# Other places for the conv blocks' exit from PSUM, for table loads and copies of ScalarE, and for the output's scaling, in a four-layer decoder trunk

## The chip, the cores and the metric

The kernel runs on one core of one Trainium2 chip. The metric is the device time of one execution in microseconds, the median of several runs. A core has five engines with an instruction row of their own, each of which works through its row in order: TensorE (PE: matmuls), VectorE (DVE), ScalarE (ACT), GpSimd (POOL) and SyncE (SP, which here issues DMAs). They share data in SBUF and, for matmul results, in PSUM, and wait for one another through semaphores.

## The reference

What is computed is one inference step of a trunk of four layers, for 256 prompt tokens and 8 sample tokens with the same weights, in float32. Layers 0 and 3 have a short gated conv as mixer, layer 1 a pooling over several windows, layer 2 a Conformer conv; each mixer is followed by an MLP with squared ReLU. The change lies in the Conformer conv and in the last norm.

```python
def layer_norm(x, g, b):
    xf = x.astype(jnp.float32)
    mu = jnp.mean(xf, axis=-1, keepdims=True)
    var = jnp.mean(jnp.square(xf - mu), axis=-1, keepdims=True)
    y = (xf - mu) * lax.rsqrt(var + EPS)
    return (y * g.astype(jnp.float32) + b.astype(jnp.float32)).astype(x.dtype)
...
def conformer_conv_mixer(xn, state, w_pw1, b_pw1, conv_w, conv_b, ln_g, ln_b, w_pw2, b_pw2):
    ag = jnp.einsum('bld,de->ble', xn, w_pw1) + b_pw1
    a, g = jnp.split(ag, 2, axis=-1)
    buf = jnp.concatenate([state, a * jax.nn.sigmoid(g)], axis=1)
    z = causal_dwconv(buf, conv_w) + conv_b
    z = layer_norm(z, ln_g, ln_b)
    y = jnp.einsum('ble,ed->bld', jax.nn.silu(z), w_pw2) + b_pw2
    return y, buf[:, -(CONV_C_W - 1):]
...
    return rms_norm(x, norm_final_g), jnp.stack(new_a), jnp.stack(new_b), jnp.stack(new_c)
```

## The kernel before

Channels lie on the 128 partitions, so the 1024 channels are 8 blocks, and the 264 tokens (256 + 8) lie along the free axis. Every weight matrix comes from HBM as units of 1024 x 256 (`wst`). ScalarE rounds a piece of a unit to fp32r (`whi`, line 119), then VectorE or GpSimd subtracts it from the original (`wlo`, line 120, on the engine in `lo_engine`), and TensorE multiplies three times (`mm`, lines 160 to 162). `pump` puts these two steps in between other work. The order of all instructions on each engine is the order in which the Python code issues them (`manual_schedule`).

In `mixer_c` (line 827) the first pointwise product and the GLU give 8 blocks `gb`. The depthwise conv over 31 taps is split: blocks 0 to 3 are done on VectorE, tap by tap, in a PSUM accumulator (`do_taps`, line 858; the last tap and the bias come first, as a scaled copy of ScalarE, line 901), and blocks 4 to 7 on TensorE, as 64 steps `conv_step` (line 926) over matrices `mats` that hold the taps. Each of these four blocks leaves two half results in PSUM, `pairs`. `leave` (line 951) takes a block out: ScalarE copies the two halves that lie on the other partitions (`over`), VectorE adds them to the own halves (line 960). `apart` (line 967) subtracts an estimated mean, on GpSimd or VectorE, squares on ScalarE, and lets GpSimd add the blocks up into `dsum` and `qsum`; blocks 3 and 7 stay apart. Calls of all these are placed by the step number n in the loop over the 64 steps (lines 1015 to 1044).

After the loop `token_sums` (line 994) sums over the channels with matmuls against a matrix of ones, 28 or 56 columns wide: `dsum`, `qsum`, then block 3 and its square, then block 7 and its square. From these come the mean and the inverse root of each token, spread to all partitions by two small products (`wide` and `scale`, `to_channels`). `keep_clock(n)` issues n matmuls of ones by ones with no use for the result, called warm-up here; each is two passes in the trace. Then the second pointwise product starts as a `wave` over three units, whose first step needs the first normed block (`normed`, `gated`). A table load stands on ScalarE wherever the function set changes (Sigmoid, Sqrt); `root_table` asks for Sqrt early.

At the end of the kernel the squares of the last layer are summed per token, `rsqrt` gives a scale per token, and three row blocks `ys` of 128 tokens are scaled in two halves and sent out (lines 1285 to 1307).

Of the kernel before, what the change touches and what calls it, by code (L numbers as in the profile page):

```python
# [11 lines left out]
ALU = mybir.AluOpType  # L12
# [14 lines left out]
def decoder_trunk(ctx: ExitStack, tc: tile.TileContext, i, o):  # L27
# [136 lines left out]
    def psum():  # L164
        return pmm.tile([P, 512], F32, tag="mm", name="mm")
# [661 lines left out]
    def mixer_c(ready):  # L827
# [61 lines left out]
        def evac_a(e, ps):  # L889
            t1 = ps[:, :T]  # L890
            nc.vector.tensor_tensor(out=t1, in0=t1, in1=r, op=ALU.mult)
            nc.vector.scalar_tensor_tensor(
                out=gb[e][:, 30:], in0=t1, scalar=col("bpw1", e), in1=sg.pop(e), op0=ALU.add, op1=ALU.mult
            )
            later.append(lambda: out_rows.put(e, gb[e][:, 30 + T - P:]))

            def rest():
                if e < PE0:
                    if e < 3:
                        zb[e] = psum()  # L900
                    nc.scalar.activation(
                        z(e), gb[e][:, 30:30 + SEQ], AF.Identity, scale=col("ccw", 30 * 8 + e), bias=col("cb", e)
                    )
                    todo[e] = list(range(30))
                elif e < NB - 1:
                    double(e)
                if e in (0, 1, 2, 4):
                    make_mat()
                    make_mat()
                sample_sum(e)  # L910
                do_taps(4)

            return rest
# [24 lines left out]
        def first_mean():  # L938
# [9 lines left out]

            return means

        def leave(e):


            over = tmp.tile([P, SEQ], F32, tag="t1", name="over")
            for s in range(2):
                own, other = (slice(h * HALF, (h + 1) * HALF) for h in (s, 1 - s))
                nc.scalar.copy(over[own], pairs[e, s][other, 1:SEQ + 1])
            for s in range(2):
                own = slice(s * HALF, (s + 1) * HALF)
# [54 lines left out]
        total, done = sum(len(v) for v in todo.values()), 0  # L1014
        for n, step in enumerate(steps):
            conv_step(*step)
            if n == 15:
                leave(4)
                double(NB - 1)
            if n < 16:  # L1020
                make_mat(nc.scalar if n % 4 == 3 else nc.gpsimd)
            if n >= 20 and n % 3 == 0:
                run_later(1)
            want = total * max(0, n - 3) // 58
            done += do_taps(want - done, not (todo[0] or todo[1]))
            if n == 58:
                root_table()
            for at, e in ((33, 5), (49, 6)):
                if n == at:
                    leave(e)  # L1030
            if n == 8:
                assert not (todo[0] or todo[1])
                means = first_mean()
            if n == 16:
                ss = means()
            if n == 20:
                nc.vector.tensor_scalar_mul(mu, ss, 1.0 / (P * some))
# [12 lines left out]
        lo_engine[0] = nc.vector  # L1050
        pump(len(background))
        lag[0] = 0
        widths = (28, 56)
        sums = [pst.tile([P, T], F32, tag="st", name="sums"), psum()]
        few = tmp.tile([P, 4, 3], F32, tag="rs", name="few", bufs=1)
        md, v, root, rz = (few[:, k] for k in range(4))
        wide = psum()
        warm = ptp.tile([P, 512], F32, tag="tp", name="warm")
        keep_clock(5, warm)
        token_sums(sums[0], widths[0], 0, "d")  # L1060
        token_sums(sums[1], widths[1], 0, "q")
        token_sums(sums[0], widths[0], 1, "d3")
        token_sums(sums[1], widths[1], 1, "q3")
        token_sums(sums[0], widths[0], 2, "d7")
        token_sums(sums[1], widths[1], 2, "q7")
        dq = [
            ps[:, 0:9 * w].rearrange("p (b r w) -> p b r w", r=3, w=w)[:, :, :, 0] for ps, w in zip(sums, widths)
        ]
# [217 lines left out]
    for n, sq in enumerate((acc, last_square)):  # L1286
        for b, c0 in enumerate(starts):
            c = n * 3 + b
            nc.tensor.matmul(ss[:, c:c + 1], sq[:, c0:c0 + P], ones[:, 0:1], start=True, stop=True)
    run_later(NB)  # L1290
    rt = tmp.tile([P, 3], F32, tag="rt", name="rt", bufs=1)
    v, s = root_tiles(3)
    mean(v, ss[:, 0:3])
    nc.vector.scalar_tensor_tensor(out=v, in0=ss[:, 3:6], scalar=1.0 / D, in1=v, op0=ALU.mult, op1=ALU.add)
    rsqrt(v, s, rt)
    for b in range(3):
        scale = rt[:, b:b + 1]
        for h, part in enumerate((ys[b][:, 0:512], back[1, b])):
            s = slice(h * 512, (h + 1) * 512)
            if h == 0:  # L1300
                nc.vector.tensor_scalar_mul(ys[b][:, s], part, scale)
            else:
                nc.scalar.activation(ys[b][:, s], part, AF.Copy, scale=scale)
            if b < 2:
                nc.sync.dma_start(out=o["y_prompt"][0, b * P:(b + 1) * P, s], in_=ys[b][:, s])
        if b == 2:
            nc.scalar.dma_start(out=o["y_sample"].rearrange("b l d -> (b l) d"), in_=ys[b][120:128, :])


# [1 line left out]
_INS = ['x_prompt', 'x_sample', 'state_conv_a', 'state_pool', 'state_conv_c', 'norm_mix_g', 'norm_mlp_g',  # L1311
# [27 lines left out]
```

## Time and profile before

| | us |
|---|---|
| median of 3 runs | 1106.61 (1104.82 to 1107.35) |
| profiled execution, its own time | 1105.2 |
| its span | 1103.5 |
| TensorE busy | 1091.9 |
| VectorE busy | 744.9 |
| ScalarE busy | 613.1 |
| GpSimd busy | 199.4 |

The span is what the profiler saw from the first to the last instruction; the execution's own time lies 1.7 us above it. All times in the rows below are us from the span's start. A row of a timeline has the start, the time covered, engine, line, operation and operands; `x6` means six such instructions in one row, and in brackets stands how long the engine was idle before it and what released it. Instructions of one engine overlap a little, so the step from one start to the next is the price of one, not its own duration. PE lists every float32 matmul as two passes.

### The profile page before, as it was taken

Reading aid. Unit: us, or ns where it says so; the run is one execution under the profiler, and the core shown is the slowest. Engines: PE = TensorE matmul, PEld = TensorE weight load, DVE = VectorE, ACT = ScalarE, POOL = GpSimd, SP = SyncE. Lnnn points to the kernel's source line nnn. Section 1 sums busy time; section 2 is a strip of 40 time slices with the busy share of each in tenths; the row PEclk is TensorE's granted clock in tenths of the full one; section 3 lists DMA queues with packets and bytes.
Section 4 is the critical chain, followed back from the end, with each engine's and each line's share of the span. In section 5 each row is a group of like instructions: output and inputs, shape, how many; then the busy total and the mean of one; then the engine's idle time right before and its main releaser. Section 6 shows DMA issues by size and latency. Waiting matters only on the chain.

```text
span 1103.5 us, 21936 instructions
## 1 busy us (share of the span) xinstructions
PE 1091.9 (99%) x8801; PEld 1082.6 (98%) x8801; DVE 744.9 (68%) x1461; ACT 613.1 (56%) x1301; POOL 199.4 (18%) x364
## 2 busy tenths in 40 slices
PE   9999999999999999999999999999999999999997
PEld 8999999999999999999988999999999999999996
DVE  6888865566569657766986696466668678646731
ACT  6565663565458545555855585365545467535642
POOL 4212520100220001314993200000111120000010
PEclk9999999999999999999998999999999999999999
DMA  7766756655507666654531186555546565565511
GB/s 244 255 207 198 251 194 174 179 183 168 176 5 244 216 197 193 198 169 148 181 83 39 39 265 223 163 190 192 169 141 218 165 188 191 172 190 175 192 39 40
DMA packets 182790, 189.10 MB, mean 171 GB/s; under 512 B 3439, under 2 KB 181015, under 8 KB 182664
## 3 DMA queue, kind: packets, MB, share of 16 engines
q1 hardware_dynamic: 182288, 185.86, 53.5%
q0 software_dynamic: 384, 1.81, 0.5%
q8 instruction: 69, 1.13, 0.4%
q14 instruction: 33, 0.27, 0.1%
q10 hardware_dynamic: 16, 0.03, 0.0%
HBM read 186.27 MB, written 2.89 MB: 171 GB/s over the span
## 4 chain that ended last, share of the span: by engine, by line
PE 91%; DVE 4%; POOL 2%; ACT 2%; DMA 1%; issue 0%; SPq 0%; DVEq 0%; POOLq 0%; ACTq 0%
PE mm L160 28%; PE mm L162 28%; PE mm L161 28%; DVE mm L858 2%; POOL wlo L120 1%; PE mm L348 1%; PE mm L346 1%; PE mm L349 1%; DMA vrows<-in_c_b_pw_dram 1%; POOL mat L814 1%; PE mm L1186 1%; ACT mat L821 0%; PE sums L999 0%; PE mm L999 0%; PE mm L507 0%
## 5 line engine op out<-in xcount | busy, mean ns | idle before, releaser
L119 ACT CAST whi<-wst 128x512 fp32r<-128x512 f32 x692 | 387.0, 616 | 250.3 <-PE mm L161 233.5
L120 DVE TENSOR_TENSOR wlo<-wst,whi 128x512 fp32r<-128x512 f32 x652 | 433.5, 709 | 102.5 <-ACT whi L119 94.8
L160 PE MATMUL mm<-xh,whi 128*128 128x264 f32 x1512 | 433.2, 287 | 0.0
L162 PE MATMUL mm<-xh,wlo 128*128 128x264 f32 x1512 | 429.6, 284 | 0.3 <-DVE wlo L120 0.2
L161 PE MATMUL mm<-xl,whi 128*128 128x264 f32 x1512 | 428.0, 283 | 0.0
L160 PE MATMUL mm<-uh,whi 128*128 128x264 f32 x1168 | 332.5, 285 | 0.0
L162 PE MATMUL mm<-uh,wlo 128*128 128x264 f32 x1168 | 331.6, 284 | 0.0
L161 PE MATMUL mm<-ul,whi 128*128 128x264 f32 x1168 | 331.2, 284 | 0.0
L161 PEld LDWEIGHTS mm<-xl,whi 128*128 128x128 f32 x1512 | 285.1, 189 | 0.2
L162 PEld LDWEIGHTS mm<-xh,wlo 128*128 128x128 f32 x1512 | 284.2, 188 | 0.7 <-DVE wlo L120 0.7
L160 PEld LDWEIGHTS mm<-xh,whi 128*128 128x128 f32 x1512 | 284.4, 188 | 0.3
L160 PEld LDWEIGHTS mm<-uh,whi 128*128 128x128 f32 x1168 | 220.0, 188 | 0.2 <-DVE xall L541 0.2
L161 PEld LDWEIGHTS mm<-ul,whi 128*128 128x128 f32 x1168 | 219.7, 188 | 0.0
L162 PEld LDWEIGHTS mm<-uh,wlo 128*128 128x128 f32 x1168 | 219.5, 188 | 0.0
L248 POOL TENSOR_TENSOR acc<-acc,sq 128x264 f32<-128x264 f32 x62 | 53.6, 865 | 551.0 <-ACT sq L247 550.2
L1132 DVE SCALAR_TENSOR_TENSOR t<-mm,r 128x264 f32<-128x264 f32 x128 | 54.8, 428 | 63.3 <-PE mm L162 63.1
L230 ACT CAST uh<-u 128x264 fp32r<-128x264 f32 x144 | 59.5, 413 | 33.1 <-DVE u L596 29.1
L1138 ACT ACTIVATE u<-t 128x264 f32<-128x264 f32 x128 | 54.0, 422 | 39.8 <-DVE t L1132 39.8
L232 DVE TENSOR_TENSOR ul<-u,uh 128x264 fp32r<-128x264 f32 x144 | 62.3, 433 | 0.3
L539 DVE TENSOR_TENSOR xall<-mm,xall 128x264 f32<-128x264 f32 x48 | 20.6, 430 | 59.1 <-PE mm L162 59.1
L235 ACT ACTIVATE xh<-xall,pv 128x264 fp32r<-128x264 f32 x56 | 28.9, 515 | 46.0 <-DVE xall L539 29.9
L120 POOL TENSOR_TENSOR wlo<-wst,whi 128x512 fp32r<-128x512 f32 x40 | 50.7, 1294 | 16.0 <-ACT whi L119 16.0
(230 smaller groups left out, 727.3 us busy)
## 6 DMA issues: line engine op xcount, KB each, us to landing
wst<-in_mlp_w_dram SPq DMA_DIRECT2D x128, 1024.0 KB, 5.6
wst<-in_a_w_in_dram SPq DMA_DIRECT2D x23, 1024.0 KB, 5.3
wst<-in_c_w_pw_dram SPq DMA_DIRECT2D x12, 1024.0 KB, 5.6
wst<-in_a_w_out_dram SPq DMA_DIRECT2D x8, 1024.0 KB, 5.1
xin<-in_x_prompt_dram SPq DMA_DIRECT2D x2, 512.0 KB, 6.7
wst<-in_b_w_group_dram SPq DMA_DIRECT2D x1, 1024.0 KB
out_y_prompt_dram<-ys SPq DMA_DIRECT2D x4, 256.0 KB, 2.2
stc<-in_state_conv_c_dram SPq DMA_DIRECT2D x2, 480.0 KB, 7.4
```

The costliest lines, as they stand in the source:

```text
L119: nc.scalar.copy(hi[:, k:k + 2], st[:, k:k + 2])
L120: (nc.gpsimd if u == 3 or (u, k) in ((0, 2), (0, 6)) else lo_engine[0]).tensor_tensor(out=lo[:, k:k + 2], in0=st[:, k:k + 2], in1=hi[:, k: ...
L160: nc.tensor.matmul(ps[:, :n], hi[:, k, s], xh[:, :n], start=first, stop=False)
L161: nc.tensor.matmul(ps[:, :n], hi[:, k, s], xl[:, :n], start=False, stop=False)
L162: nc.tensor.matmul(ps[:, :n], lo[:, k, s], xh[:, :n], start=False, stop=last)
L230: nc.scalar.copy(h, src)
L232: lambda: nc.vector.tensor_tensor(out=l, in0=src, in1=h.bitcast(F32), op=ALU.subtract)
L235: nc.scalar.activation(h, src, AF.Copy, scale=g)
L248: nc.gpsimd.tensor_tensor(out=acc, in0=acc, in1=sq, op=ALU.add)
L858: nc.vector.scalar_tensor_tensor(out=z(e), in0=gb[e][:, t:t + SEQ], scalar=col("ccw", t * 8 + e), in1=z(e), op0=ALU.mult, op1=ALU.add,)
L1132: nc.vector.scalar_tensor_tensor(out=t1, in0=ps[:, :T], scalar=0.0, in1=r, op0=ALU.max, op1=ALU.mult)
L1138: nc.scalar.activation(u, t1, AF.Square)
```

## The change

It does six things:

- The first tap of blocks 0 to 3 is done by VectorE.
- `leave` is cut in two: `come_over`, ScalarE's copies, right after a block's last matmul (n = 15, 31, 47, 63); `leave`, VectorE's adds, at n = 16, 40, 55 and after the loop. Block 5's `apart` moves from n = 38 to 40.
- VectorE's taps are spread to be done sooner (`want`).
- From n = 32 the weight subtractions go to VectorE instead of GpSimd; two are left there.
- The Sqrt table is asked for at n = 49 instead of 58, the Sigmoid table right behind the root; all sums are 56 columns wide, in two PSUM tiles of the other pool, and the warm-up matmuls stand 2, 1, 1, 3, 6 instead of 5, 4, 7.
- At the end the two halves of the last sums have a PSUM tile each; VectorE scales four of the six half blocks and ScalarE two, ScalarE sends one out itself, and SP sends the sample.

```diff
@@ mixer_c, evac_a
-                    nc.scalar.activation(
-                        z(e), gb[e][:, 30:30 + SEQ], AF.Identity, scale=col("ccw", 30 * 8 + e), bias=col("cb", e)
+                    nc.vector.tensor_scalar(
+                        out=z(e), in0=gb[e][:, 30:30 + SEQ], scalar1=col("ccw", 30 * 8 + e), scalar2=col("cb", e),
+                        op0=ALU.mult, op1=ALU.add,
                     )
@@ mixer_c
-        def leave(e):
-            over = tmp.tile([P, SEQ], F32, tag="t1", name="over")
+        def come_over(e):
+            over_[e] = tmp.tile([P, SEQ], F32, tag="t1", name="over")
             for s in range(2):
                 own, other = (slice(h * HALF, (h + 1) * HALF) for h in (s, 1 - s))
-                nc.scalar.copy(over[own], pairs[e, s][other, 1:SEQ + 1])
+                nc.scalar.copy(over_[e][own], pairs[e, s][other, 1:SEQ + 1])
+        def leave(e):
+            over = over_.pop(e)
...
             conv_step(*step)
-            if n == 15:
+            for at, e in ((15, 4), (31, 5), (47, 6), (63, 7)):
+                if n == at:
+                    come_over(e)
+            if n == 16:
                 leave(4)
                 double(NB - 1)
...
-            want = total * max(0, n - 3) // 58
+            want = total * (n + 1) // 60
             done += do_taps(want - done, not (todo[0] or todo[1]))
-            if n == 58:
+            if n == 49:
                 root_table()
-            for at, e in ((33, 5), (49, 6)):
+            for at, e in ((40, 5), (55, 6)):
                 if n == at:
                     leave(e)
...
-            for at, e in ((22, 4), (24, 0), (26, 1), (38, 5), (55, 6)):
+            for at, e in ((22, 4), (24, 0), (26, 1), (40, 5), (55, 6)):
                 if n == at:
                     apart(e)
...
+            if n == 32:
+                lo_engine[0] = nc.vector
             if n in (36, 40, 44, 46):
                 pump(1, False)
...
-        widths = (28, 56)
-        sums = [pst.tile([P, T], F32, tag="st", name="sums"), psum()]
+        width = 56
+        sums = [psum(), psum()]
...
-        keep_clock(5, warm)
-        token_sums(sums[0], widths[0], 0, "d")
...
+        keep_clock(2, warm)
+        for at, e in enumerate(("", "3", "7")):
+            for ps, what in zip(sums, "dq"):
+                token_sums(ps, width, at, what + e)
+            if at < 2:
+                keep_clock(1, warm)
...
         rsqrt(v, root, rz)
+        nc.scalar.activation(scratch, ones[:, 0:1], AF.Sigmoid)
         nc.scalar.copy(mu, wide[:, :T])
-        keep_clock(4, warm)
+        keep_clock(3, warm)
         scale = pst.tile([P, T], F32, tag="st", name="scale")
         to_channels(scale, rz)
-        keep_clock(7, warm)
+        keep_clock(6)
@@ the end of the kernel
-    ss = pst.tile([P, T], F32, tag="st", name="st")
+    ss = [pst.tile([P, T], F32, tag="st", name="st"), ptp.tile([P, 512], F32, tag="tp", name="st2")]
...
-    for b in range(3):
...
+    for b, h in ((0, 0), (0, 1), (1, 0), (1, 1), (2, 0), (2, 1)):
+        out, part, scale = ys[b][:, h * 512:(h + 1) * 512], back[1, b] if h else ys[b][:, 0:512], rt[:, b:b + 1]
+        scalar = (b, h) in ((0, 1), (2, 1))
...
```

VectorE's order around block 5's adds, before. `d5` is block 5's result, `gb2` and `gb3` are the inputs of the taps of blocks 2 and 3:

```order
L858 SCALAR_TENSOR_TENSOR mm_6798<-gb3_6680,pv_95,mm_6798 128x256
L858 SCALAR_TENSOR_TENSOR mm_6984<-gb2_6679,pv_95,mm_6984 128x256
L960 SCALAR_TENSOR_TENSOR d5_7411<-mm_7503,pv_95,over_7569 64x256
L960 SCALAR_TENSOR_TENSOR d5_7411<-mm_7529,pv_95,over_7569 64x256
L858 SCALAR_TENSOR_TENSOR mm_6798<-gb3_6680,pv_95,mm_6798 128x256
```

And after the change:

```order
L120 TENSOR_TENSOR wlo_7393<-wst_7213,whi_7392 128x512
L858 SCALAR_TENSOR_TENSOR mm_6984<-gb2_6679,pv_95,mm_6984 128x256
L858 SCALAR_TENSOR_TENSOR mm_6798<-gb3_6680,pv_95,mm_6798 128x256
L858 SCALAR_TENSOR_TENSOR mm_6984<-gb2_6679,pv_95,mm_6984 128x256
L858 SCALAR_TENSOR_TENSOR mm_6798<-gb3_6680,pv_95,mm_6798 128x256
L966 SCALAR_TENSOR_TENSOR d5_7411<-mm_7498,pv_95,over_7565 64x256
L966 SCALAR_TENSOR_TENSOR d5_7411<-mm_7532,pv_95,over_7565 64x256
L120 TENSOR_TENSOR wlo_7393<-wst_7213,whi_7392 128x512
L858 SCALAR_TENSOR_TENSOR mm_6984<-gb2_6679,pv_95,mm_6984 128x256
```

Five more taps than before stand ahead of this piece; the two `wlo` subtractions, rows of GpSimd before, now stand in it, the second right behind the adds of block 5.

ScalarE's order at the same place, before. `L980` squares a block into `gb`, `L957` copies a block's halves over, `L119` is the cast that a `wlo` subtraction needs:

```order
L119 CAST whi_7392<-wst_7213 128x512
L980 ACTIVATE gb5_6682<-d5_7411 128x264
L119 CAST whi_7392<-wst_7213 128x512
L957 COPY over_7617<-mm_7564 64x256
L957 COPY over_7617<-mm_7593 64x256
L980 ACTIVATE gb6_6683<-d6_7412 128x264
L980 ACTIVATE gb2_6679<-d2_7408 128x264
L268 ACT_TABLE_LOAD
L268 ACTIVATE scratch_86<-ones_85 128x1
```

And after the change:

```order
L119 CAST whi_7392<-wst_7213 128x512
L986 ACTIVATE gb5_6682<-d5_7411 128x264
L119 CAST whi_7392<-wst_7213 128x512
L959 COPY over_7613<-mm_7569 64x256
L959 COPY over_7613<-mm_7588 64x256
L268 ACT_TABLE_LOAD
L268 ACTIVATE scratch_86<-ones_85 128x1
L986 ACTIVATE gb6_6683<-d6_7412 128x264
L986 ACTIVATE gb2_6679<-d2_7408 128x264
```

The casts, the square of block 5 and the copies of block 6 stand as they stood; the Sqrt table has moved ahead of the squares of blocks 6 and 2.

TensorE's order from the end of the conv to the mean's broadcast, before:

```order
L1186 MATMUL warm<-ones 128x128 x5
L999 MATMUL sums<-ones,dsum 128x28 x3
L999 MATMUL mm<-ones,qsum 128x56 x3
L999 MATMUL sums<-ones,d_7409 128x28 x3
L999 MATMUL mm<-ones,gb_6680 128x56 x3
L999 MATMUL sums<-ones,d_7413 128x28 x3
L999 MATMUL mm<-ones,gb_6684 128x56 x3
L1006 MATMUL mm<-ident,few 128x128 x2
L1006 MATMUL mm<-ident,few 128x32
L1186 MATMUL warm<-ones 128x128 x4
```

And after the change:

```order
L1195 MATMUL warm<-ones 128x128 x2
L1005 MATMUL mm<-ones,dsum 128x56 x3
L1005 MATMUL mm<-ones,qsum 128x56 x3
L1195 MATMUL warm<-ones 128x128
L1005 MATMUL mm<-ones,d_7409 128x56 x3
L1005 MATMUL mm<-ones,gb_6680 128x56 x3
L1195 MATMUL warm<-ones 128x128
L1005 MATMUL mm<-ones,d_7413 128x56 x3
L1005 MATMUL mm<-ones,gb_6684 128x56 x3
L1012 MATMUL wide<-ident,few 128x128 x2
L1012 MATMUL wide<-ident,few 128x32
L1195 MATMUL warm<-ones 128x128 x3
```

The same six groups of sums stand there, wider, with fewer warm-up matmuls ahead of them and two between them.

## Rows read from the trace of the kernel before

**Rows 1.** The page: busy time by engine (share of the span, instructions), and one group of instructions.
```profile
PE 1091.9 (99%) x8801; PEld 1082.6 (98%) x8801; DVE 744.9 (68%) x1461; ACT 613.1 (56%) x1301; POOL 199.4 (18%) x364
...
L120 DVE TENSOR_TENSOR wlo<-wst,whi 128x512 fp32r<-128x512 f32 x652 | 433.5, 709 | 102.5 <-ACT whi L119 94.8
```

**Rows 2.** TensorE's timeline, end of the conv to the wave: start us, us, operation, [idle before].
```profile
582.79 1.28 PE L1186 MATMUL warm<-ones 128*128 128x128 f32 x10
585.53 0.85 PE L999 MATMUL sums<-ones,dsum 128*128 128x28 f32 x6 [1.47 <-POOL dsum L988]
...
587.08 1.44 PE L999 MATMUL sums<-ones,d 128*128 128x28 f32 x6
...
592.19 1.74 PE L1006 MATMUL mm<-ident,few 128*128 128x128 f32 x6
593.86 2.08 PE L1186 MATMUL warm<-ones 128*128 128x128 f32 x8
595.73 1.62 PE L1006 MATMUL scale<-ident,few 128*128 128x128 f32 x6
...
599.66 0.39 PE L348 MATMUL mm<-uh,whi 128*128 128x264 f32 x1 [0.51 <-ACT uh L230]
```

**Rows 3.** Busy time by stretch: us, then each engine; PEclk is the granted clock.
```profile
587.00:590.00 3.00, 3.00 (x15) 2.93 (x15) 1.42 (x4) 1.58 (x4) 0.00 (x0) 0.53 0.03 5
...
596.00:598.00 2.00, 2.00 (x12) 1.71 (x12) 0.57 (x2) 0.15 (x1) 2.00 (x4) 0.65 0.00 0
599.60:602.00 2.40, 2.34 (x18) 2.23 (x18) 1.38 (x5) 2.40 (x7) 0.00 (x0) 1.00 0.00 0
```

**Rows 4.** Groups of VectorE's instructions, GLU stretch: busy us, mean ns, idle before, releaser.
```profile
L858 DVE SCALAR_TENSOR_TENSOR mm<-gb,pv,mm 128x256 f32<-128x256 f32 x58 | 24.3, 482 | 3.3 <-ACT mm L901 3.2
```

**Rows 5.** VectorE's timeline, conv blocks and norm.
```profile
572.45 1.00 DVE L960 SCALAR_TENSOR_TENSOR d<-mm,pv,over 64x256 f32<-64x256 f32 x2 [2.64 <-ACT over L957]
573.48 6.36 DVE L858 SCALAR_TENSOR_TENSOR mm<-gb,pv,mm 128x256 f32<-128x256 f32 x16
579.87 1.00 DVE L960 SCALAR_TENSOR_TENSOR d<-mm,pv,over 64x256 f32<-64x256 f32 x2
...
594.45 0.77 DVE L1084 TENSOR_TENSOR d<-d,mm 128x264 f32<-128x264 f32 x2 [0.61 <-ACT mu L1077]
```

**Rows 6.** ScalarE's timeline, conv blocks and norm.
```profile
572.83 0.62 ACT L119 CAST whi<-wst 128x512 fp32r<-128x512 f32 x1
...
576.11 0.60 ACT L119 CAST whi<-wst 128x512 fp32r<-128x512 f32 x1
...
585.13 1.28 ACT L268 ACT_TABLE_LOAD   x1
586.42 0.20 ACT L268 ACTIVATE scratch<-ones 128x1 f32<-128x1 f32 x1
...
592.83 0.21 ACT L257 ACTIVATE few<-few 128x3 f32<-128x3 f32 x1 [2.89 <-DVE few L1075]
593.97 0.38 ACT L1077 COPY mu<-mm 128x264 f32<-128x264 f32 x1 [0.93 <-PE mm L1006]
594.37 1.28 ACT L1093 ACT_TABLE_LOAD   x1
```

**Rows 7.** GpSimd's timeline, conv blocks.
```profile
574.86 0.73 POOL L975 TENSOR_TENSOR d<-d,mu 128x256 f32<-128x256 f32 x1
...
580.95 0.73 POOL L975 TENSOR_TENSOR d<-d,mu 128x256 f32<-128x256 f32 x1 [2.45 <-DVE d L960]
...
583.32 0.22 POOL L978 TENSOR_TENSOR d<-zs,mu 128x8 f32<-128x8 f32 x1
584.74 0.74 POOL L988 TENSOR_TENSOR dsum<-dsum,d 128x264 f32<-128x264 f32 x1 [1.20 <-DVE d L973]
```

**Rows 8.** The timeline of the output's tail.
```profile
1095.30 0.16 DVE L264 TENSOR_SCALAR rv<-st 128x3 f32<-128x3 f32 x1 [1.44 <-PE st L1289]
...
1097.24 1.83 SPq L1305 DMA_DIRECT2D out_y_prompt_dram<-ys  x4
```

More of the change, by code (lines that the diff above doesn't have):

```diff
@@ L949, in first_mean @@
             return means
-        def leave(e):
-            over = tmp.tile([P, SEQ], F32, tag="t1", name="over")
+        over_ = {}
+        def come_over(e):
+            over_[e] = tmp.tile([P, SEQ], F32, tag="t1", name="over")
             for s in range(2):
                 own, other = (slice(h * HALF, (h + 1) * HALF) for h in (s, 1 - s))
-                nc.scalar.copy(over[own], pairs[e, s][other, 1:SEQ + 1])
+                nc.scalar.copy(over_[e][own], pairs[e, s][other, 1:SEQ + 1])
+        def leave(e):
+            over = over_.pop(e)
             for s in range(2):
@@ L1052, in mixer_c @@
         lag[0] = 0
-        widths = (28, 56)
-        sums = [pst.tile([P, T], F32, tag="st", name="sums"), psum()]
+        width = 56
+        sums = [psum(), psum()]
         few = tmp.tile([P, 4, 3], F32, tag="rs", name="few", bufs=1)
         md, v, root, rz = (few[:, k] for k in range(4))
-        wide = psum()
-        warm = ptp.tile([P, 512], F32, tag="tp", name="warm")
-        keep_clock(5, warm)
-        token_sums(sums[0], widths[0], 0, "d")
[L1061 to L1068, printed above, removed]
+        wide = ptp.tile([P, 512], F32, tag="tp", name="wide")
+        warm = pst.tile([P, T], F32, tag="st", name="warm")
+        keep_clock(2, warm)
[4 more added lines that the diff above has]
+                keep_clock(1, warm)
+        dq = [ps[:, 0:9 * width].rearrange("p (b r w) -> p b r w", r=3, w=width)[:, :, :, 0] for ps in sums]
         nc.vector.tensor_reduce(out=md, in_=dq[0], op=ALU.add, axis=mybir.AxisListType.X)
@@ L1284, in decoder_trunk @@
     mlp(last_ready)
-    ss = pst.tile([P, T], F32, tag="st", name="st")
-    for n, sq in enumerate((acc, last_square)):
+    ss = [pst.tile([P, T], F32, tag="st", name="st"), ptp.tile([P, 512], F32, tag="tp", name="st2")]
+    for ps, sq in zip(ss, (acc, last_square)):
         for b, c0 in enumerate(starts):
-            c = n * 3 + b
-            nc.tensor.matmul(ss[:, c:c + 1], sq[:, c0:c0 + P], ones[:, 0:1], start=True, stop=True)
+            nc.tensor.matmul(ps[:, b:b + 1], sq[:, c0:c0 + P], ones[:, 0:1], start=True, stop=True)
     run_later(NB)
@@ L1292, in decoder_trunk @@
     v, s = root_tiles(3)
-    mean(v, ss[:, 0:3])
-    nc.vector.scalar_tensor_tensor(out=v, in0=ss[:, 3:6], scalar=1.0 / D, in1=v, op0=ALU.mult, op1=ALU.add)
+    mean(v, ss[0][:, 0:3])
+    nc.vector.scalar_tensor_tensor(out=v, in0=ss[1][:, 0:3], scalar=1.0 / D, in1=v, op0=ALU.mult, op1=ALU.add)
     rsqrt(v, s, rt)
-    for b in range(3):
[L1297 to L1307, printed above, removed]
+    for b, h in ((0, 0), (0, 1), (1, 0), (1, 1), (2, 0), (2, 1)):
+        out, part, scale = ys[b][:, h * 512:(h + 1) * 512], back[1, b] if h else ys[b][:, 0:512], rt[:, b:b + 1]
+        scalar = (b, h) in ((0, 1), (2, 1))
+        if scalar:
+            nc.scalar.activation(out, part, AF.Copy, scale=scale)
+        else:
+            nc.vector.tensor_scalar_mul(out, part, scale)
+        if b < 2:
+            (nc.scalar if scalar else nc.sync).dma_start(
+                out=o["y_prompt"][0, b * P:(b + 1) * P, h * 512:(h + 1) * 512], in_=out
+            )
+    nc.sync.dma_start(out=o["y_sample"].rearrange("b l d -> (b l) d"), in_=ys[2][120:128, :])
 _INS = ['x_prompt', 'x_sample', 'state_conv_a', 'state_pool', 'state_conv_c', 'norm_mix_g', 'norm_mlp_g',
```

## The prediction

> **What bounds the kernel now.** I read the page's busy shares first: TensorE is busy 99% of the span, VectorE and ScalarE far less [rows 1]. So a change of microseconds matters only where TensorE waits or runs slowly. Next came TensorE's timeline, searched for idle time and for matmuls slower than their neighbours. All of that lies in one stretch inside the Conformer mixer, between the last conv matmul and the wave of the second pointwise product. There TensorE does ten warm-up passes, idles 1.47 us until GpSimd's `dsum` is ready, does six groups of token sums, and only at 599.66 starts the wave [rows 2]. The windows view shows what the waiting costs besides: the granted clock is 0.53 of full, its lower level, from 587 on, and 0.65 between 596 and 598, where it rises again [rows 3]. The price of one sum group is therefore of two kinds: 0.78 us (585.53 to 587.08 holds two) and 1.28 us (587.08 to 592.19 holds four) [rows 2]. Four engines feed this stretch, so I then read VectorE, ScalarE and GpSimd row by row there: the question is which of them delivers `dsum` last. Outside it the edits touch only the conv's first taps and the output's tail.
>
> **The first taps.** Four scaled copies of ScalarE become VectorE instructions. In the GLU stretch VectorE waited 3.2 us in total for those copies [rows 4], and one VectorE instruction of this size costs about 0.48 us as a tap does there [rows 4], so 4 x 0.48 = 1.9 us replaces 3.2 us of waiting. TensorE waits for nothing there. I cost it at nothing: the matmuls of the GLU hide it, and VectorE enters the conv stretch when TensorE's last GLU block releases it, as before.
>
> **VectorE through the conv blocks.** Before, VectorE stood 2.64 us waiting for block 5's copy, until 572.45; it had thus finished its earlier work at 569.81 [rows 5]. A tap costs 0.40 us (16 of them between 573.48 and 579.87) [rows 5]. The change lets VectorE do more taps before block 5, so that this wait goes; but it puts two weight subtractions, which GpSimd did before, into VectorE's row, one four taps ahead of block 5's adds and one right behind them. Each needs a cast of ScalarE, and ScalarE's order there has not changed at all.
> - VectorE reaches the first subtraction 5 taps later than it stopped before: 569.81 + 5 x 0.40 = 571.81. The cast it needs ends at 572.83 + 0.62 = 573.45 [rows 6]. It waits 1.6 us, then works 0.71 us [rows 1]: 574.2. Four taps and the two adds of block 5 (1.03 us, 572.45 to 573.48 [rows 5]) bring it to 576.8.
> - The second subtraction needs a cast that stands on ScalarE behind the square of block 5, which needs GpSimd's subtraction of block 5, which needs the two adds that VectorE has just done. GpSimd's start to the cast's end took 574.86 to 576.71 [rows 6, 7], that is 1.85 us; with 0.1 us of hand-over VectorE stands from 576.8 to 578.8, then works to 579.5.
> - 15 taps later, at 585.5, it begins block 6's adds. Before that was 579.87 [rows 5]: 5.6 us later.
> - GpSimd starts on block 6 1.08 us after those adds begin (579.87 to 580.95), and is free for the last `dsum` add 2.59 us after that (583.32 + 0.22) [rows 5, 7]. That gives 585.5 + 1.1 + 2.6 = 589.2, and with the 0.74 us of the add itself [rows 7] 590.0. Before, TensorE's first sum began at 585.53. So the sums start **4.5 us later**. Blocks 3 and 7 follow within 2 us on VectorE and ScalarE, while TensorE is in the earlier groups, so they add no wait.
>
> TensorE's own conv ends no earlier than before: its matmuls do not depend on this. At most block 7's first bank comes 0.5 us late. So TensorE idles some 6 us where it idled 1.47.
>
> **The sums and the norm.** At the lower clock six groups and two inserted warm-up pairs (4 passes of 1.87/8 = 0.23 us [rows 2]) take 6 x 1.28 + 0.94 = 8.6 us: from 590.0 to 598.6 instead of 592.19. That is 6.4 us late. I price the wider sums as the old ones, since the groups of 28 and of 56 columns lie together in those 5.11 us and the 56 column ones have their own share in it. Then the mean's broadcast takes 1.67 us (592.19 to 593.86), three warm-up pairs 1.40 us where four took 1.87, and the scale 1.62 us [rows 2]: 4.7 us, against 5.16 us before, so the scale ends 5.9 us late. From there to the wave nothing changes (597.35 to 599.66, 2.3 us [rows 2]).
>
> The moved Sigmoid table is worth nothing here. Its load of 1.28 us began at 594.37 [rows 6], and the first Sigmoid could not start before the scale's end at 595.73 + 1.62 = 597.35 [rows 2]. In the new order it stands ahead of the copy of the mean, so that VectorE's first subtraction ends about 3.5 us after the sums (0.64 to the root, 592.19 to 592.83, its 0.21, then 1.28 + 0.20 + 0.38, and 0.77 on VectorE [rows 2, 5, 6]); that is inside the 4.7 us. The Sqrt table's load likewise began in idle time before and after. The row says that the next instruction starts 0.01 us behind the load (585.13 + 1.28, then 586.42 [rows 6]). [...]
>
> **The tail.** The final mean no longer waits for the last squares, since the two sums have a PSUM tile each; one small VectorE instruction of 0.16 us and its gap leave the path [rows 8]. The output blocks go out by two queues. The SP issues took 1.83 us for four, 0.46 us each [rows 8]; three of them plus the small sample now stand there, and ScalarE issues one ahead of its second block. One issue more or less on the path bounds it: a loss of 0.5 to a gain of 0.6 us; I take a gain of 0.2, the one instruction.
>
> **Sum.** +5.9 - 0.2 = +5.7 us on the profiled execution's own 1105.2 us (span 1103.5): **1110.9 us**. That execution is 1.4 us under the median 1106.61 of the three runs, which spread over 2.5 us; by the median it would be 1112.3. I stay with the former as the point, and let the range hold both.
>
> **Rivals.**
> 1. *The clock comes back during the sums.* For it: all groups are now 56 columns wide and warm-up pairs stand between them. Against it: TensorE was busy without a gap from 587 to 596 and stayed at the lower level [rows 2, 3]. [...] If it comes back after three groups: 590.0 + 3 x 1.28 + 0.47 + 0.26 + 3 x 0.78 = 596.9. At the full clock the mean's copy behind the table load then sets the end: 3.5 + 2.3 us to the wave, 602.7, so +3.0 - 0.2: **1108.0**.
> 2. *The clock never falls.* For it: the first sums of before still ran at full speed, right after 1.47 us of idling. Against it: four times that idle time. Sums to 590.0 + 6 x 0.78 + 0.5 = 595.2, wave at 601.0: +1.3 - 0.2, **1106.3**, no measurable change.
> 3. *The clock is still low when the wave begins.* Its first 18 matmuls took 2.34 us [rows 3]; at half speed another 2.3 us: **1113**.
> 4. *Faster: VectorE does not stand at the subtractions*, because ScalarE's casts are early. Then the change does what its title says: both waits (1.6 and 2.0 us) vanish, `dsum` is ready at 586.4, and if the clock also holds, the wave starts at 586.4 + 5.2 + 5.8 = 597.4: -2.3 - 0.2, **1102.7**. It decides at one point: whether the second cast ends before VectorE's adds of block 5. By the instruction order it cannot, since it waits for their result; hence little chance.
>
> **How the numbers follow.** Forecast 0.55; rival 1 0.17; rival 2 0.11; rival 3 0.12; rival 4 0.05. About 0.2% (2.2 us) is what a measurement can tell from no change. Slower by more: the forecast, rival 3 and three fifths of rival 1, 0.77. Within: rival 2, the lower part of rival 1, 0.17. Faster: rival 4 and what I overlooked, 0.06. The range reaches from rival 2, less what the profile's run lies off, at 1105.8, to rival 3 at 1113.2; it leaves out rival 4 and the ends of the others.
>
> **What would show it.** In the profile after, VectorE should stand about 1.6 us before the first weight subtraction and about 2 us right behind block 5's adds, with ScalarE's cast as the releaser; block 6's adds should begin near 585.5; TensorE should idle some 6 us for `dsum` and begin the sums near 590; their groups should take 1.28 us at a granted clock of 0.5, and the wave begin near 605.5. The forecast is wrong if VectorE shows no idle time at the subtractions, if the sums' rows show the full clock, or if the wave starts before 602.

## The result, and the profile after

| | before | after |
|---|---|---|
| median | 1105.71 us (4 runs) | **1113.06 us** (4 runs, 1112.12 to 1113.81) |
| profiled execution's span | 1103.5 us | 1110.4 us |

The ratio is 1.0063 (95% interval 1.0050 to 1.0077), 5.5 to 8.5 us slower. Repeated later beside other runs it was 1.0046 (1.0032 to 1.0060). The forecast was +5.7 us, 1110.9, in a range of 1105.8 to 1113.2: the measured median lies 2.2 us above the point and 0.14 us below the range's upper end.

TensorE's timeline of the changed kernel, where [rows 2] stood before:

```profile
583.97 0.61 PE L1195 MATMUL warm<-ones 128*128 128x128 f32 x4
590.70 1.53 PE L1005 MATMUL mm<-ones,dsum 128*128 128x56 f32 x6 [6.12 <-POOL dsum L994]
592.02 1.49 PE L1005 MATMUL mm<-ones,qsum 128*128 128x56 f32 x6
...
599.27 1.74 PE L1012 MATMUL wide<-ident,few 128*128 128x128 f32 x6
600.95 1.65 PE L1195 MATMUL warm<-ones 128*128 128x128 f32 x6
602.65 1.78 PE L1012 MATMUL scale<-ident,few 128*128 128x128 f32 x6
604.37 2.68 PE L1195 MATMUL mm<-ones 128*128 128x128 f32 x12
607.14 0.39 PE L348 MATMUL mm<-uh,whi 128*128 128x264 f32 x1
```

The wait for `dsum` is 6.12 us instead of 1.47, and from 590.70 almost to the wave all of TensorE's work runs slowly (1.49 us for the group `qsum`, at a granted clock of 0.50). The windows view of the same stretch, where [rows 3] stood, says why (the third number from the end is the granted clock):

```profile
587.00:592.00 5.00, 1.30 (x6) 1.30 (x7) 4.12 (x10) 2.00 (x5) 4.25 (x9) 0.76 0.00 0
592.00:596.00 4.00, 4.00 (x21) 4.00 (x21) 0.16 (x1) 0.42 (x1) 0.00 (x0) 0.50 0.01 4
604.00:606.00 2.00, 2.00 (x9) 1.94 (x10) 1.38 (x3) 0.61 (x1) 2.00 (x4) 0.50 0.00 0
606.00:608.00 2.00, 1.91 (x14) 1.72 (x13) 1.66 (x4) 1.32 (x3) 0.35 (x1) 0.84 0.00 0
```

The clock falls inside the idle time (1.00 up to 589, 0.79 from 589 to 590, 0.50 from 590) and is back at 1.00 only about half a microsecond ahead of the wave (0.50 up to 606.5, 0.85 from 606.5 to 607, 1.00 from 607). VectorE's timeline, where [rows 5] stood:

```profile
566.99 5.96 DVE L858 SCALAR_TENSOR_TENSOR mm<-gb,pv,mm 128x256 f32<-128x256 f32 x15
574.05 0.69 DVE L120 TENSOR_TENSOR wlo<-wst,whi 128x512 fp32r<-128x512 f32 x1 [1.11 <-issue]
574.66 1.66 DVE L858 SCALAR_TENSOR_TENSOR mm<-gb,pv,mm 128x256 f32<-128x256 f32 x4
576.23 0.99 DVE L966 SCALAR_TENSOR_TENSOR d<-mm,pv,over 64x256 f32<-64x256 f32 x2
579.19 1.08 DVE L120 TENSOR_TENSOR wlo<-wst,whi 128x512 fp32r<-128x512 f32 x1 [1.96 <-ACT whi L119]
580.30 5.97 DVE L858 SCALAR_TENSOR_TENSOR mm<-gb,pv,mm 128x256 f32<-128x256 f32 x15
586.18 0.99 DVE L966 SCALAR_TENSOR_TENSOR d<-mm,pv,over 64x256 f32<-64x256 f32 x2
...
604.94 0.81 DVE L1105 TENSOR_SCALAR gb<-d,pv 128x264 f32<-128x264 f32 x1
605.86 0.79 DVE L1114 TENSOR_TENSOR d<-gb,sgm 128x264 f32<-128x264 f32 x1
```

ScalarE's and GpSimd's, where [rows 6, 7] stood:

```profile
573.35 0.62 ACT L119 CAST whi<-wst 128x512 fp32r<-128x512 f32 x1
578.22 0.42 ACT L986 ACTIVATE gb<-d 128x264 f32<-128x264 f32 x1 [4.26 <-POOL d L984]
578.55 0.60 ACT L119 CAST whi<-wst 128x512 fp32r<-128x512 f32 x1
...
600.14 1.28 ACT L1085 ACT_TABLE_LOAD   x1
601.44 0.20 ACT L1085 ACTIVATE scratch<-ones 128x1 f32<-128x1 f32 x1
601.55 0.36 ACT L1086 COPY mu<-wide 128x264 f32<-128x264 f32 x1
```
```profile
577.30 0.72 POOL L981 TENSOR_TENSOR d<-d,mu 128x256 f32<-128x256 f32 x1 [3.17 <-DVE d L966]
...
589.90 0.74 POOL L994 TENSOR_TENSOR dsum<-dsum,d 128x264 f32<-128x264 f32 x1
...
602.05 4.30 POOL L1095 TENSOR_TENSOR d<-d,mu 128x264 f32<-128x264 f32 x6 [10.39 <-ACT mu L1086]
```

The ring is to be seen: VectorE's adds of block 5 (576.23) release GpSimd (577.30), that releases the square (578.22), behind it stands the second cast (578.55), and VectorE stands for it until 579.19, in front of the 15 taps that stand ahead of block 6's adds. For the first wait the row names no releaser (`issue`); the cast that this subtraction needs ends at 573.35 + 0.62 = 573.97, 0.08 us ahead of its start. The output's tail, where [rows 8] stood, VectorE and then SyncE's queue:

```profile
1100.90 0.43 DVE L539 TENSOR_TENSOR xall<-mm,xall 128x264 f32<-128x264 f32 x1 [2.49 <-PE mm L162]
1101.79 0.16 DVE L264 TENSOR_SCALAR rv<-st 128x3 f32<-128x3 f32 x1 [0.46 <-PE st L1297]
...
1104.52 1.39 SPq L1313 DMA_DIRECT2D out_y_prompt_dram<-ys  x3
1106.01 0.89 SPq L1316 DMA_DIRECT2D out_y_sample_dram<-ys  x1
```

**Where the 6.9 us of the spans lie.** The conv's first matmul in both kernels, and the last addition to the residual before:

```profile
553.72 7.53 PE L929 MATMUL mm<-two,mat 128*128 128x257 f32 x34
...
1093.43 0.43 DVE L539 TENSOR_TENSOR xall<-mm,xall 128x264 f32<-128x264 f32 x1 [2.49 <-PE mm L162]
```
```profile
554.89 7.53 PE L930 MATMUL mm<-two,mat 128*128 128x257 f32 x34
```

Before, the conv's first matmul started at 553.72, the wave at 599.66, the last addition to the residual (line 539) at 1093.43, and the span ended at 1103.5. After, they are 554.89, 607.14, 1100.90 and 1110.4. So 1.17 us arise ahead of the conv, 6.31 between conv and wave, nothing from there to the last addition, and the tail is 0.57 shorter. The 1.17 us are not put down to the change. In this execution, and not in that of before, the clock fell in the pooling mixer, whose code is the same, which by an estimate is worth 1.6 us (10 us at 0.84):

```profile
310.00:320.00 10.00, 10.00 (x69) 9.66 (x68) 7.14 (x24) 3.51 (x9) 3.61 (x5) 0.84 0.00 0
```

The execution of the repeated run has 1.00 there, but 0.50 from 25 to 28 us, and its conv began at 554.59. With 1.00 from 310 to 320 the conv began at 552.64 in run 2 below, a changed kernel, and at 553.72 before; in runs 3, 5, 6, 11 and 12, which have nothing of the change ahead of the conv and 0.83 to 0.86 there, it began between 554.98 and 557.32. **The change itself is thus 6.31 - 0.57 = +5.7 us.**

### The profile page after: what moved, and what is told of

The parts are those of the page before. It is cut to its first block, busy times and chain, and to the rows that moved or that the text cites. A ratio compares the mean times of both kernels' runs of the same rounds, so it can differ in the third digit from the quotient of the medians.

```text
span 1110.4 us, 21924 instructions
## 1 busy us (share of the span) xinstructions
PE 1095.1 (99%) x8795; PEld 1085.6 (98%) x8795; DVE 748.2 (67%) x1468; ACT 610.5 (55%) x1297; POOL 196.0 (18%) x362
## 4 chain that ended last, share of the span: by engine, by line
PE 91%; DVE 4%; POOL 3%; ACT 1%; issue 1%; DVEq 0%; POOLq 0%; ACTq 0%
PE mm L160 28%; PE mm L162 28%; PE mm L161 28%; DVE mm L858 2%; POOL wlo L120 1%; PE mm L348 1%; PE mm L346 1%; PE mm L349 1%; DVE wlo L120 1%; PE mm L1005 1%; POOL mat L814 1%; PE mm L1195 1%; POOL d L981 0%; PE mm L507 0%; PE st L278 0%
## 5 line engine op out<-in xcount | busy, mean ns | idle before, releaser
L119 ACT CAST whi<-wst 128x512 fp32r<-128x512 f32 x692 | 386.9, 616 | 250.3 <-PE mm L161 233.5
L120 POOL TENSOR_TENSOR wlo<-wst,whi 128x512 fp32r<-128x512 f32 x38 | 48.1, 1298 | 15.1 <-ACT whi L119 15.1
```

The costliest lines, as they stand in the source:

```text
L119: nc.scalar.copy(hi[:, k:k + 2], st[:, k:k + 2])
L120: (nc.gpsimd if u == 3 or (u, k) in ((0, 2), (0, 6)) else lo_engine[0]).tensor_tensor(out=lo[:, k:k + 2], in0=st[:, k:k + 2], in1=hi[:, k: ...
```

## The experiments

Because such falls come and go, each run is read twice: by its median and by three stretches of its profile. "Sums" and "wave" are the starts of the first sum and of the wave behind the conv's first matmul, "tail" is from the last addition to the end of the span. The last column counts the runs with a mean granted clock of 0.995 or more. They are taken as those where the clock stayed up through the norm, because among the profiled executions it stayed up in three, with means of 0.995 and 0.996, and fell in ten, with 0.993 or less. The three are those of runs 1, 4 and 8, so their "wave" is that of a clock that held.

| kernel | median, us | ratio (95%) | sums | wave | tail | held |
|---|---|---|---|---|---|---|
| before | 1106.0 to 1106.35 | 1 | 31.81 | 45.94 | 10.07 | 2 of 90 |
| after | 1113.06 | 1.0063 (1.0050, 1.0077) | 35.81 | 52.25 | 9.50 | 0 of 4 |
| after, again | 1112.24 | 1.0046 (1.0032, 1.0060) | 35.74 | 52.18 | 9.47 | 0 of 5 |
| after, subtractions on GpSimd | 1100.72 | 0.9954 (0.9939, 0.9970) | 31.08 | 41.34 | 9.51 | 7 of 8 |
| after, second pair one step earlier | 1107.89 | 1.0021 (1.0012, 1.0031) | 33.50 | 49.94 | 9.54 | 0 of 12 |
| before, subtractions on VectorE | 1108.23 | 1.0021 (1.0013, 1.0030) | 33.45 | 47.62 | 10.02 | 0 of 12 |
| after, 24 warm-up pairs | 1109.91 | 1.0029 (1.0013, 1.0045) | 35.69 | 45.96 | 9.52 | 3 of 12 |
| before, sums 56 wide | 1106.36 | 1.0003 (0.9994, 1.0013) | 31.82 | 45.86 | 10.05 | 0 of 12 |
| before, pairs 2, 1, 1 | 1106.47 | 1.0002 (0.9993, 1.0010) | 31.81 | 47.78 | 10.06 | 0 of 11 |
| run 1, Sigmoid's load behind the copy | 1104.39 | 0.9974 (0.9960, 0.9987) | not read | not read | not read | 5 of 11 |
| the same, idle time filled | 1101.27 | 0.9962 (0.9948, 0.9976) | 31.09 | 40.88 | 9.47 | 5 of 7 |
| before, new norm block | 1106.56 | 0.9994 (0.9981, 1.0008) | 31.68 | 44.12 | 10.04 | 3 of 12 |
| after on GpSimd, old norm block | 1104.76 | 0.9976 (0.9966, 0.9987) | 31.07 | 43.65 | 9.55 | 2 of 12 |
| before, new tail | 1104.72 | 0.9991 (0.9981, 1.0000) | 31.79 | 46.06 | 9.49 | 0 of 11 |

**1. The subtractions back on GpSimd.**
```diff
-            if n == 32:
-                lo_engine[0] = nc.vector
```


> The changed kernel with the weight subtractions of the conv stretch back on GpSimd; all else as changed. Theory (VectorE's stalls at the two subtractions make dsum late): VectorE shows no idle time there, block 6's adds begin about 26.7 us behind the conv's first matmul (31.3 in the changed kernel, 26.2 before), TensorE idles about 1.4 us for dsum instead of 6.1, the first sums run at the full clock, and the median is 1105 to 1108. Rival (the wider sums, the warm-up pairs between them and the moved table cost the time): TensorE's idle time shrinks but the wave starts no more than 2 us earlier, median above 1111.

Measured: 1100.72 us, 11.5 to 12.3 us below the changed kernel's two medians and faster than before. TensorE's timeline of this run:
```profile
585.49 0.61 PE L1193 MATMUL warm<-ones 128*128 128x128 f32 x4
587.50 0.88 PE L1005 MATMUL mm<-ones,dsum 128*128 128x56 f32 x6 [1.40 <-POOL dsum L994]
...
592.04 1.00 PE L1012 MATMUL wide<-ident,few 128*128 128x128 f32 x6
...
597.76 0.39 PE L348 MATMUL mm<-uh,whi 128*128 128x264 f32 x1 [1.22 <-ACT uh L230]
```
The conv starts at 556.42 here. The idle time is 1.40 us, and the sums take 4.54 us instead of 8.57, at the full clock (1.00 in all windows from 586 to 608). Two lines of the change carry its whole loss; the rest of it is a gain of some 5 us in these eight runs, seven of which held the clock. The theory holds in its place: block 6's adds stand 26.56 us behind the conv's first matmul, without idle time ahead of them. The median is below the 1105 to 1108 expected, since the clock now stayed up to the wave. Of the 10.9 us by which the changed kernel's wave is later than this one's, 4.7 are the later sums, and 6.2 arise from there on, at a clock of 0.50 until 606.5 where this run has 1.00.

**2. The second cast and subtraction one step earlier.**
```diff
-            if n in (36, 40, 44, 46):
+            if n in (36, 39, 44, 46):
```


> The changed kernel with only the second of the two casts and subtractions placed one conv step earlier (n = 39), which puts the cast ahead of block 5's square on ScalarE and the subtraction ahead of block 5's adds on VectorE. Theory (the wait on a cast that itself waits for those adds): the 1.96 us wait goes, block 6's adds begin about 2.2 us earlier, dsum too, the median is about 1110.9. Rival (it is the 1.4 to 1.8 us of VectorE's work on the subtractions, not the wait): block 6's adds move by under 0.7 us, median 1112.4 or more.

VectorE's timeline:
```profile
571.82 0.69 DVE L120 TENSOR_TENSOR wlo<-wst,whi 128x512 fp32r<-128x512 f32 x1 [1.12 <-issue]
...
573.61 0.69 DVE L120 TENSOR_TENSOR wlo<-wst,whi 128x512 fp32r<-128x512 f32 x1
574.21 0.48 DVE L858 SCALAR_TENSOR_TENSOR mm<-gb,pv,mm 128x256 f32<-128x256 f32 x1
574.60 0.99 DVE L966 SCALAR_TENSOR_TENSOR d<-mm,pv,over 64x256 f32<-64x256 f32 x2
575.63 5.97 DVE L858 SCALAR_TENSOR_TENSOR mm<-gb,pv,mm 128x256 f32<-128x256 f32 x15
581.63 1.00 DVE L966 SCALAR_TENSOR_TENSOR d<-mm,pv,over 64x256 f32<-64x256 f32 x2
```
The second wait is gone, the first is still there. Block 6's adds stand 28.99 us behind the conv's first matmul (552.64) where they stood at 31.29: 2.30 us, as expected, and the wave comes 2.31 us earlier. The clock fell as before (0.72 from 584 to 586, then 0.50 up to 600): no run held it, and the median, 1107.89 (1110.9 expected), stays above that of before. So the second wait is some 2 of the 4.73 us by which the changed kernel's sums are later than run 1's; the first wait is 1.11, and the rest, 1.72, the work (574.05 to 574.66, 579.19 to 580.30). The medians differ by 4.4 to 5.2 us, more than this stretch holds; in run 2's profile the conv began 1.95 to 2.25 us earlier, ahead of anything that the edit touches.

**3. The kernel before with the subtractions on VectorE.**
```diff
+            if n == 32:
+                lo_engine[0] = nc.vector
```


> The kernel before with one edit: the two weight subtractions of the conv stretch on VectorE. There the adds of block 5 stand at n = 33, ahead of both. Theory: VectorE waits for no cast, only its work of 2 x 0.7 us is added; block 6's adds begin about 1.4 us later than the 26.2 us behind the conv's first matmul, TensorE idles about 2.9 us, the median is 1107 to 1108.5. Rival (moving the subtractions costs the whole loss wherever the adds stand): block 6's adds 5 us later, median above 1111.

Measured 1108.23, the sums 1.64 us later than before, the wave 1.68. The same two lines make the sums 1.64 us later where block 5's adds stand ahead of both subtractions, and 4.73 where they stand between them: the order adds the two waits, some 3 us. The other 6 of the 11 us at the wave go with the lower clock; the kernel before has lost that in nearly all its runs (2 of 90 held), and run 3 had 0.50 from 590 to 600 too, so it can't show its price.

**4. The idle time filled.**
```diff
-        keep_clock(2, warm)
+        keep_clock(24, warm)
```


> The changed kernel with 24 warm-up pairs instead of 2 behind the conv, which fill TensorE's 6.1 us of idle time; dsum is as late as before. Theory A (the idle time lets the clock fall): the six sum groups run at the full clock at 0.75 us each, the wave starts about 5 us earlier, median about 1108. Theory B (the narrow sums let it fall whatever stands ahead of them, as between 587 and 596 in the kernel before): only the first two or three groups are at the full clock, the wave starts 1 to 2 us earlier, median 1111 to 1112.

The profiled execution, one of three whose clock held, shows theory A, all sums at the full clock (1.00 in all windows from 582 to 608) though `dsum` is as late as in the changed kernel:
```profile
584.20 5.52 PE L1195 MATMUL warm<-ones 128*128 128x128 f32 x48
590.82 0.88 PE L1005 MATMUL mm<-ones,dsum 128*128 128x56 f32 x6 [1.10 <-POOL dsum L994]
...
595.36 1.00 PE L1012 MATMUL wide<-ident,few 128*128 128x128 f32 x6
```
In it the wave starts 6.3 us earlier. But the median, 1109.91, lies between the theories, the 12 runs reach from 1105.27 (mean clock 0.996) to 1113.01 (0.989), and 9 of them have a clock under 0.995. With the filling, which leaves 1.10 us of idle time, the clock held in three executions and not in the other nine: the length of the idle time ahead of the sums does not decide alone.

**5 and 6. The kernel before with wider sums, and with its pairs between the groups.**
```diff
-        widths = (28, 56)
-        sums = [pst.tile([P, T], F32, tag="st", name="sums"), psum()]
+        widths = (56, 56)
+        sums = [psum(), psum()]
```


> The kernel before with one edit: all six sum groups 56 columns wide, both sums in PSUM tiles of the other pool. Before, the clock fell as the third group (28 columns wide) began. Theory (the wider sums keep the clock up): the groups run at 0.7 us each to the end, the wave starts about 42 us behind the conv's first matmul instead of 45.9, median 1102 to 1103, mean clock of most runs 0.995 or more. Rival (the width is no matter): the wave at 45.9, median 1105.5 to 1106.5.

```diff
-        keep_clock(5, warm)
+        keep_clock(2, warm)
...
+        keep_clock(1, warm)
         token_sums(sums[0], widths[0], 1, "d3")
...
+        keep_clock(1, warm)
         token_sums(sums[0], widths[0], 2, "d7")
```


> The kernel before with one edit: the warm-up pairs around the sums stand 2, 1, 1 instead of 5 (two ahead, one between the blocks' groups), widths 28 and 56 as before. Theory (the pairs between the groups keep the clock up): the wave starts about 42.5 us behind the conv's first matmul, median 1102.5 to 1103.5. Rival (they don't, they only add their time): the wave at 46.4 to 46.9, median 1106 to 1107.

Both medians are the rivals', 1106.36 and 1106.47, and none of the 23 runs has a mean clock of 0.995. In run 6 the wave came 1.84 us later than before, more than its rival's 0.5 to 1.0: with fewer warm-up passes TensorE idled 2.13 us for `dsum`, and the first sums ran slowly already (1.23 us from the first to the second group, 0.70 before), at a clock of 0.78 from 586 to 588 and 0.50 behind. In the run with wider sums it fell where TensorE waited a second time, for block 7 (1.00 from 588 to 590, 0.51 from 590 to 592):
```profile
589.17 0.83 PE L999 MATMUL mm<-ones,gb 128*128 128x56 f32 x6
590.86 1.53 PE L999 MATMUL mm<-ones,d 128*128 128x56 f32 x6 [0.86 <-DVE d L975]
```
With the earlier exit of the conv blocks that wait does not exist, neither in run 1 nor in run 10, where the clock fell all the same in ten of 12 runs.

**7 and 8. Run 1 with the Sigmoid table's load behind the mean's copy; the same with the idle time filled.**
```diff
-        nc.scalar.activation(scratch, ones[:, 0:1], AF.Sigmoid)
         nc.scalar.copy(mu, wide[:, :T])
+        nc.scalar.activation(scratch, ones[:, 0:1], AF.Sigmoid)
```


> The changed kernel with the subtractions back on GpSimd, and the Sigmoid table's load behind the copy of the mean instead of ahead of it. Theory (at the full clock the mean's copy behind the load sets when the norm begins): VectorE's subtraction of the mean begins about 1.2 us earlier behind the sums, the wave starts 0.4 to 0.8 us earlier than the 41.3 us of the run without this edit, median about 1100.2. Rival (the scale sets it anyway): the wave no more than 0.1 us earlier, same median of 1100.7.

```diff
-        keep_clock(2, warm)
+        keep_clock(6, warm)
...
-        keep_clock(3, warm)
+        keep_clock(3)
```


> As the run beside it (subtractions on GpSimd, Sigmoid's load behind the copy), with 6 warm-up pairs instead of 2 behind the conv, which fill most of the 1.4 us of idle time, and the warm-up ahead of the scale in a PSUM tile of its own. Theory A (idle time lets the clock fall): all runs have a mean clock of 0.995 or more, none is above 1102.5, the scale's first matmul no longer waits 0.35 us, median about 1099.5. Theory B (filling does not hold the clock): as many runs with a clock under 0.993 as beside it, median the same within 0.5 us.

Run 7 has a median of 1104.39 (ratio 0.9974, 0.9960 to 0.9987), above what either side expected; its profiled execution took 1174 us at a granted clock of 0.848, so its stretches can't be read. The clock held in 5 of the 11 others. Run 8 measured 1101.27 (0.9962, 0.9948 to 0.9976), held in 5 of 7, and its timeline shows what the two edits do together: VectorE subtracts the mean 1.52 us behind the sums' end, run 1 2.69; the scale starts 0.82 us behind the start of the six warm-up passes ahead of it, in run 1 0.99; the wave starts 5.25 us behind the sums' end instead of 5.72. The 0.47 us are there, the runs can't show them beside the scatter of the clock. Neither theory of run 8 holds as put: against A, three of its runs are above 1102.5 and two have a clock under 0.995; against B, none is under 0.993, where run 7 has six. Neither version beats run 1 clearly.

**9. The changed kernel again.**

> The changed kernel itself once more, beside the kernel before on the same chip, with the runs that follow. Theory (the loss is the later dsum, and behind 6 us of idle time the clock is always down during the sums): every run has a mean clock of 0.991 or less, the wave starts 52.2 us behind the conv's first matmul (45.9 before), the tail is 0.55 us shorter, so the ratio is near 1.0052 and the median 1111 to 1113. Rival (something else of the change, outside that stretch, costs 1 to 2 us more): ratio 1.0063 or more and a later first conv matmul in every trace of a changed kernel.

1112.24 us, wave at 52.18, tail 9.47, all five clocks between 0.988 and 0.990, ratio 1.0046: the theory. The rival's later first conv matmul is not there in run 2.

**10 and 11. Exit of the conv blocks and norm block apart.** Run 10 is run 1 with the norm block of before; run 11 is the kernel before with the new one (widths, PSUM tiles, pairs, Sigmoid's load), both from the diff of the change.

> The changed kernel with the subtractions on GpSimd and the whole norm block (widths, PSUM tiles, warm-up pairs, Sigmoid's load) as before. Theory A (the earlier exit of the conv blocks is what holds the clock in most runs): the wave about 41 to 42 us behind the conv's first matmul in a run with a held clock, most runs at a mean clock of 0.995, median near 1101. Theory B (the new norm block holds it): the clock falls in every run, wave near 45, median 1104.5 to 1105.5.

> The kernel before with the whole new norm block (widths 56, two PSUM tiles, pairs 2, 1, 1, 3, 6, Sigmoid's load ahead of the mean's copy), the exit of the conv blocks as before. Theory A: as the clock needs the earlier exit, it falls in every run, the wave starts 46 to 47 us behind the conv's first matmul, median 1105.8 to 1107. Theory B: the clock holds in most runs, wave near 42.5, median 1102 to 1103.

Neither does it alone: the clock held in 2 and in 3 of 12 runs, together (run 1) in 7 of 8. Run 10 has theory B's median, 1104.76, but two runs that held, and a wave at 43.65. Run 11 has theory A's median, 1106.56, but three runs that held, and a wave between the two theories', at 44.12; its runs go from 1101.53 (0.997) to 1109.04 (0.989).

**12. The kernel before with the new tail** (the last hunk of the diff alone).

> The kernel before with only the new scaling and sending of the output. Theory (one small VectorE instruction and the wait for the last squares leave the path, and the sends are better spread): from the last addition to the residual to the end of the span 9.5 us instead of 10.07, ratio near 0.9995, median about 1105.5, not to be told from no change by the runs alone. Rival (the send on ScalarE ahead of its second block costs what the rest gains): 10.0 us or more.

The tail takes 9.49 us: 0.58 less. The runs (0.9991, up to 1.0000) agree.

## Why the prediction was right

- **The first taps** cost nothing, as forecast: TensorE is busy all 13 us from 540 to 553 in both profiles, and VectorE no longer waits for ScalarE there (1.2 us from 531 to 553 before, none after).
- **The two stalls** were forecast at 1.6 and 2.0 us and measured 1.11 and 1.96. The first was shorter because ScalarE's copies of block 5 start 0.65 us earlier behind the conv's first matmul. The second subtraction then held VectorE's row for 1.11 us, priced at 0.71. Block 6's adds came 5.14 us later (forecast 5.6), the sums 4.0 (4.5).
- **The idle time** (6.12 us, forecast some 6), the clock (0.50) and the sums (8.57 us, forecast 8.6) came as the forecast had them. Rivals 1 and 2, a clock that comes back or never falls, did not occur in the two profiles, and the mean clocks of all nine runs (0.986 to 0.990) give no sign of them. Rival 3 came close in the first profile, where the clock returned some 0.5 us ahead of the wave, and came true in part in the repeated run's: there it returned 1.6 us behind the wave's start (its matmuls step by 0.22 us up to 608.26 and by 0.12 from 608.46), which cost 0.5 us up to the last addition, where rival 3 had 2.3.
- **From the sums to the scale's end** the forecast was 0.46 us less than before, for one warm-up pair fewer. Measured: no gain. The scale's weight load waited 0.35 us for the last warm-up pass, which now writes into a PSUM tile with the scale's tag; with a tile of its own for the warm-up, the scale of run 8 starts 0.17 us sooner behind it than run 1's.
- **From the scale to the wave** the forecast was no change; it took 0.40 us more (604.43 to 607.14). Line 1105 took 0.81 us there, the same instruction before (line 1096) 0.42. GpSimd's six subtractions of the mean ran beside it, from 602.05 to 606.35; line 1114 took 0.79 us from 605.86 on, partly beside them, and 0.44 and 0.43 behind them. But before, GpSimd (594.49 to 598.87) ran beside the 0.42 us as well, and in run 12, where the Sigmoid load was not moved, the same instruction took 1.03 us, and scale to wave 2.57 us instead of 2.31. What makes the 0.4 us is thus not shown, nor that the moved load, priced at nothing, costs them by delaying GpSimd.
- **The tail** was forecast at -0.2, in bounds of -0.6 to +0.5; it is -0.57. 0.2 of it is the instruction that left the path (from the last addition to the root's last step 2.91 us instead of 3.10), the scaling and the sends are the rest.
- **Sum**: 4.0 + 1.9 + 0 + 0.4 - 0.6 = 5.7. The errors, half a microsecond each, cancel: each term is right to about that, and that their sum meets the forecast to a tenth is luck. The medians moved by 7.35 us, by 5.9 in the repeated run; what they have above 5.7 is not explained by the forecast's terms.
- **Rival 4**, priced at 1102.7, has its nearest case in run 1, 1100.7. But run 1 takes the subtractions out of VectorE's row, waits and work, and rival 4 leaves the work there. That its condition could not be met in this order was right: the 1.96 us wait stands behind block 5's adds.

The rows of the 0.4 us: VectorE and GpSimd before, then VectorE in run 12.

```profile
597.85 0.42 DVE L1096 TENSOR_SCALAR gb<-d,pv 128x264 f32<-128x264 f32 x1
...
594.49 4.38 POOL L1086 TENSOR_TENSOR d<-d,mu 128x264 f32<-128x264 f32 x6 [7.99 <-ACT mu L1077]
```
```profile
599.18 1.03 DVE L1096 TENSOR_SCALAR gb<-d,pv 128x264 f32<-128x264 f32 x1
```

The table load itself: ScalarE's next instruction starts 0.02 us behind its end (600.14 + 1.28, then 601.44), as in [rows 6], where it is 0.01.

## What to carry to other kernels

When work is moved to another engine, write down what each moved instruction waits for and what that producer itself stands behind. Two subtractions of 0.7 us, one of which waits for a cast that waits, over two engines, for VectorE's own adds, made the sums here 4.7 us later, 3.1 of it waiting. Where TensorE's clock fell with it, the wave came 10.9 us later than in the run without them, whose clock held. Placed behind those adds, the same two made the sums 1.6 us later. Judge a large bundle by its parts: here two lines turned a gain of 5 us into a loss of 5 to 7.

## What was not expected of the hardware

The clock's fall in one and the same kernel comes and goes by execution. Work on TensorE did not end it at once: the changed kernel's TensorE was busy for 15.24 of the 15.30 us from 590.70 to 606, at 0.50 throughout. Nor did work ahead of the sums keep it off in most executions: with 24 warm-up pairs there the clock held in 3 of 12 runs.

What decides is not shown and stays open. Run 1 held in 7 of 8 runs and run 8 in 5 of 7, but run 7, which differs from run 1 only behind the sums, in 5 of 11. Less idle time does not settle it: run 10 idles 0.72 us for `dsum` where run 1 idles 1.40, waits no second time within the sums, and held in 2 of 12. Its clock fell within them (1.00 from 588 to 590, 0.87 from 590 to 592, 0.50 from 592):

```profile
588.22 0.85 PE L1005 MATMUL sums<-ones,dsum 128*128 128x28 f32 x6 [0.72 <-POOL dsum L994]
...
590.97 0.97 PE L1005 MATMUL sums<-ones,d 128*128 128x28 f32 x6
591.76 1.51 PE L1005 MATMUL mm<-ones,gb 128*128 128x56 f32 x6
```

Runs 1 to 4, 5 to 8 and 9 to 12 were also made on three different chips. The kernel before held in 1 of 31, 0 of 30 and 1 of 29 runs on them, but that the chip has a share in the other counts is not excluded.

The pooling mixer's fall (0.83 to 0.86 from 310 to 320 in ten of the 13 profiles read, 1.00 in three) is by an estimate worth up to 1.7 us (10 us at 0.83), and the one near 25 us 1.5 (3 us at 0.50 in run 9), so a change of one is better read from a stretch of the profile than from the runs.
